# RMSNorm and a QKV projection: spent weight storage as output buffers, zero matmuls among the first transposes, a divided last product

## Chip, cores and metric

The kernel runs on one core of one Trainium2 chip. The metric is the device time of one launch in microseconds (us).

## The reference

Rows of x are divided by their root mean square, multiplied by gamma, and projected by a weight matrix.

```python
# x: (8, 1024, 768) float32, gamma: (768,), w_qkv: (768, 2304), eps = 1e-5
rms = np.sqrt(np.mean(x ** 2, axis=-1, keepdims=True) + eps)
x_norm = x / rms * gamma
return np.matmul(x_norm, w_qkv).astype(np.float32)
```

## The kernel before

The 8192 rows of x are 64 tiles of 128 rows. The inner dimension of 768 is six k-blocks of 128, and the 2304 output columns are three chunks `c` of 768.

**Start.** The weights arrive in 16 pieces (`load_w`). `conv` multiplies them by gamma and rounds them into one large bfloat16 tile, `w_b` (128 partitions x 6 x 2304, 27,648 bytes a partition). Tiles 0 to 3 of x are done in the plain way while the weights come in: `load_x`, `stat` (square sum and root on ScalarE), `cast` to bfloat16 on VectorE, `tr` (six transposes on TensorE into PSUM), `cp` (back to SBUF), `mm` (matmuls 512 or 256 columns wide against `w_b`, line 516), `evac` and `store`. `gamma_in` turns gamma into a column layout with one small transpose (line 549) and copies it to `g_sb` (line 550). `idle(n, nl)` issues n matmuls of zeros, nl columns wide, into a PSUM tile that nobody reads (line 555).

**Scaling.** For each chunk, `bound` and `fold` find the largest weight, `bound_tr`, `bound_top`, `bound_all` and `scales` make one scale of it and spread it over the partitions by way of TensorE (lines 585 and 595), and `quad` and `tsum` make eight scaled float16 blocks of weights, each 3 k-blocks by 384 columns. After the `quad`s of chunk 2 nothing reads `w_b` any more.

**The rest.** Tiles 4 to 63 are taken in pairs `p` = 2 to 31. A pair and a chunk form a 2x2 by 2x2 block product done with seven block products (the Winograd form of Strassen's scheme) in place of eight. `pstat`, `prms`, `precip` and `pcast` normalise a tile and round it to float16 (line 648), `pxbar` transposes it by DMA (for a few early tiles `ptr` does it on TensorE), and `osum` makes the four sums of blocks of x (line 666). `product` is three matmuls 384 columns wide (line 686), accumulated in one of three PSUM banks "a", "b", "c" of the pair and chunk. `hold` copies an intermediate sum to SBUF (lines 693 and 695), `join` adds a held sum to a bank and writes a part of the output tile (VectorE, line 704), and `last` writes the fourth part (ScalarE, line 708). `pstore` sends a part or a whole output tile of 768 columns to memory (SyncE's queue, line 714).

**Buffers.** `outp` holds 12 output tiles `ot` of 1024 float32, 4096 bytes a partition; `result` takes a new one for each tile and chunk. PSUM is a pool of eight tiles `pm` of one bank each. A buffer that is taken anew waits until everything that used it last is done, for an output tile its store.

**Order.** Nothing is reordered by a scheduler. `PLAN` is a list, written out, of (time, operation, arguments). The operations are called in order of these times, and each engine and queue runs its own instructions in the order of the calls; the times have no other effect. From pair 15 on (`STEADY`) the list is made by a loop with `when`. The last chunk of the last pair (`end`) has an order of its own:

```python
            for i, u in ((1, 0), (5, 1), (2, 7.5 if end else 2), (6, 4), (3, 5), (7, 7 if end else 10), (4, 8.5 if end else 13)):
                when(u, product, p, c, i)
```

The first entries of the list put `gamma_in` and six zero matmuls behind the first loads, and then the transposes of tiles 2, 1, 3 and 0, as x arrives.

Of the kernel before, what the change touches and what calls it, by code (L numbers as in the profile page):

```python
# [19 lines left out]
    (0.000, "load_x", 2), (4.040, "stat", 2), (4.041, "cast", 2, "DVE"), (4.042, "load_x", 1), (5.240, "stat", 1),  # L20
    (5.241, "load_x", 3), (5.242, "cast", 1, "DVE"), (5.243, "load_x", 0), (5.530, "recip", 2), (5.531, "load_w", 4),
    (5.532, "load_w", 1), (5.533, "load_w", 0), (5.534, "gamma_in"), (5.535, "idle", 6, 512), (5.536, "tr", 2),
    (8.470, "conv", 4, 5, "POOL"), (8.471, "cp", 2, "DVE"), (8.472, "cast", 3, "DVE"), (9.150, "conv", 1, 2, "POOL"),
    (9.151, "tr", 1), (9.152, "tr", 3), (9.153, "recip", 1), (9.154, "cast", 0, "DVE"), (9.155, "cp", 1, "ACT"),
    (9.156, "tr", 0), (9.157, "load_w", 3), (9.158, "cp", 0, "DVE"), (9.310, "mm", 1, 0, "5"), (9.311, "stat", 3),
    (9.526, "mm", 2, 0, "5"), (9.742, "mm", 0, 0, "5"), (9.743, "load_w", 2), (9.744, "load_w", 6),
    (9.745, "recip", 3), (9.990, "mm", 0, 0, "2"), (10.206, "mm", 1, 0, "2"), (10.451, "conv", 0, 0, "DVE"),
# [5 lines left out]
    (14.418, "load_w", 8), (14.419, "conv", 6, 3, "ACT"), (14.420, "mm", 0, 0, "01"), (14.421, "mm", 2, 0, "012"),  # L33
# [6 lines left out]
    (18.420, "mm", 3, 512, "45"), (18.421, "load_x", 5), (18.544, "bound_tr", 0), (18.545, "evac", 1, 512, "ACT"),  # L40
# [4 lines left out]
    (20.510, "mm", 3, 1024, "23"), (20.511, "scales", 0), (20.512, "evac", 3, 0, "DVE"),  # L45
    (20.942, "mm", 2, 1024, "23"), (21.374, "mm", 1, 1024, "45"), (21.375, "quad", 0, "b22", "ACT"),
    (21.376, "quad", 0, "b11", "POOL"), (21.377, "bound", 1, 1, "DVE"), (21.805, "mm", 2, 1024, "01"),
    (22.237, "mm", 3, 1024, "01"), (22.238, "load_w", 14), (22.239, "pstat", 4), (22.505, "pstat", 5),
    (22.669, "mm", 0, 1024, "45"), (22.670, "quad", 0, "b12", "POOL"), (22.994, "quad", 0, "b21", "POOL"),
    (23.101, "mm", 2, 512, "45"), (23.532, "mm", 1, 1024, "23"), (23.533, "bound", 1, 2, "DVE"),  # L50
    (23.534, "evac", 0, 512, "ACT"), (24.075, "prms", 2), (24.076, "mm", 2, 1024, "45"),
    (24.325, "conv", 14, 0, "ACT"), (24.755, "conv", 15, 4, "ACT"), (24.756, "mm", 3, 1024, "45"),
    (24.757, "conv", 14, 2, "POOL"), (24.758, "conv", 14, 1, "DVE"), (24.759, "fold", 1),
    (24.827, "mm", 1, 1024, "01"), (25.259, "bound_tr", 1), (25.260, "load_w", 13), (25.379, "mm", 1, 2048, "012"),
    (25.380, "precip", 2), (25.381, "evac", 2, 512, "DVE"), (25.579, "bound_top", 1), (25.707, "mm", 2, 2048, "012"),
    (26.034, "mm", 3, 2048, "012"), (26.362, "bound_all", 1), (26.363, "conv", 15, 5, "POOL"), (26.364, "pcast", 4),
    (26.365, "conv", 15, 3, "ACT"), (26.366, "evac", 3, 1024, "ACT"), (26.614, "pcast", 5),
    (26.615, "conv", 13, 4, "POOL"), (27.164, "conv", 13, 5, "DVE"), (27.165, "load_x", 7),
    (27.166, "evac", 2, 1024, "ACT"), (27.167, "pstat", 7), (27.168, "mm", 3, 2048, "345"), (27.169, "load_w", 12),
    (27.170, "mm", 2, 2048, "345"), (27.171, "load_w", 11), (27.594, "scales", 1), (27.595, "load_x", 6),  # L60
    (27.785, "evac", 2, 2048, "ACT"), (27.786, "mm", 1, 2048, "345"), (27.787, "mm", 0, 2048, "012"),
    (27.788, "load_x", 26), (28.175, "evac", 1, 2048, "ACT"), (28.315, "store", 2, 2, 2048, 256),
    (28.316, "quad", 1, "b21", "POOL"), (28.317, "mm", 0, 2048, "345"), (28.318, "tsum", 0, "t1", "DVE"),
    (28.319, "ptr", 5), (28.614, "evac", 3, 2048, "DVE"), (28.615, "ptr", 4), (29.014, "evac", 0, 2048, "DVE"),
    (29.414, "evac", 1, 1024, "DVE"), (30.074, "pcp", 4, "DVE"), (30.075, "store", 1, 2, 2048, 256),
    (30.076, "quad", 1, "b11", "ACT"), (30.077, "mm", 2, 1536, "45"), (30.078, "conv", 12, 3, "ACT"),
    (30.079, "mm", 3, 1536, "45"), (30.080, "mm", 0, 1536, "45"), (30.081, "load_x", 17), (30.574, "pcp", 5, "DVE"),
    (30.575, "mm", 1, 1536, "45"), (30.576, "conv", 11, 1, "ACT"), (30.577, "conv", 12, 2, "POOL"),
    (30.578, "mm", 0, 1024, "23"), (31.074, "bound", 2, 1, "DVE"), (31.075, "mm", 0, 1024, "01"),
    (31.429, "product", 2, 0, 1), (31.430, "conv", 11, 0, "POOL"), (31.431, "pstat", 6),  # L70
# [4 lines left out]
    (34.108, "store", 3, 2, 2048, 256), (34.109, "store", 0, 2, 2048, 256), (34.110, "quad", 1, "b12", "POOL"),  # L75
    (34.111, "mm", 1, 1536, "01"), (34.112, "mm", 3, 1536, "01"), (34.507, "mm", 1, 1536, "23"),
    (34.939, "mm", 0, 1536, "23"), (34.940, "pcast", 7), (35.370, "product", 2, 1, 1),
    (35.371, "tsum", 0, "t2", "DVE"), (35.372, "evac", 3, 1536, "ACT"), (35.904, "osum", 2, "s2", "DVE"),
    (36.058, "hold", 2, 1, "a", "p1", "ACT"), (36.364, "osum", 2, "s4", "POOL"), (36.365, "tsum", 1, "t1", "DVE"),
    (36.366, "ptr", 6), (36.367, "ptr", 7), (36.558, "pcp", 6, "ACT"), (36.559, "load_x", 8),  # L80
    (36.924, "pcp", 7, "DVE"), (37.424, "evac", 0, 1536, "DVE"), (37.425, "product", 2, 0, 5),
    (37.426, "product", 2, 1, 2), (37.427, "hold", 2, 0, "c", "p5", "ACT"), (37.428, "load_x", 13),
    (37.553, "product", 2, 0, 6), (37.878, "bound", 2, 2, "ACT"), (38.084, "tsum", 1, "t2", "DVE"),
    (38.085, "product", 3, 0, 1), (38.784, "tsum", 0, "t3", "DVE"), (38.785, "product", 2, 1, 5),
    (39.484, "osum", 2, "s3", "DVE"), (39.485, "product", 2, 0, 3), (39.804, "osum", 3, "s1", "DVE"),
    (39.805, "hold", 2, 0, "a", "u2", "ACT"), (39.806, "load_x", 15), (40.264, "osum", 3, "s2", "POOL"),
    (40.265, "tsum", 0, "t4", "DVE"), (40.266, "product", 3, 1, 1), (40.267, "hold", 2, 1, "c", "p5", "ACT"),
    (40.478, "evac", 1, 1536, "ACT"), (41.794, "osum", 3, "s3", "POOL"), (41.795, "join", 2, 1, 0, 0, "b", "p1"),
    (41.796, "product", 2, 1, 6), (41.797, "fold", 2), (41.798, "product", 2, 0, 7), (41.799, "product", 2, 1, 3),
    (41.800, "join", 2, 0, 0, 1, "c", "u2"), (42.074, "join", 2, 0, 1, 1, "a", "p5"), (42.075, "load_x", 9),  # L90
    (42.076, "product", 3, 0, 5), (42.077, "hold", 3, 1, "a", "p1", "ACT"), (42.078, "bound_tr", 2),
    (42.079, "hold", 3, 0, "a", "p1", "ACT"), (42.080, "product", 3, 1, 6), (42.081, "pstat", 9),
    (42.548, "product", 2, 0, 2), (43.035, "product", 2, 0, 4), (43.036, "bound_top", 2), (43.523, "bound_all", 2),
    (43.524, "load_x", 12), (43.643, "product", 3, 0, 6), (43.644, "hold", 2, 1, "a", "u2", "ACT"),
    (43.645, "tsum", 1, "t3", "DVE"), (43.646, "tsum", 1, "t4", "DVE"), (43.647, "hold", 3, 1, "a", "u2", "ACT"),
    (43.648, "load_x", 11), (44.244, "join", 2, 1, 0, 1, "c", "u2"), (44.794, "scales", 2),
    (44.795, "osum", 3, "s4", "POOL"), (44.796, "load_x", 10), (44.797, "product", 2, 1, 7),
    (45.114, "join", 2, 1, 1, 1, "a", "p5"), (45.664, "join", 2, 0, 0, 0, "b", "p1"), (45.665, "product", 3, 1, 7),
    (45.666, "pstat", 8), (45.667, "product", 3, 1, 2), (45.668, "product", 3, 1, 5),
    (45.669, "store", 1, 0, 0, 1024), (45.670, "hold", 3, 0, "c", "p5", "ACT"),  # L100
# [3 lines left out]
    (47.865, "prms", 4), (48.030, "product", 3, 1, 3), (48.031, "store", 3, 0, 0, 1024),  # L104
# [3 lines left out]
    (48.519, "product", 2, 2, 1), (49.064, "join", 3, 0, 1, 1, "a", "p5"), (49.065, "pstat", 10),  # L108
    (49.066, "store", 3, 1, 1024, 1024), (49.067, "product", 3, 1, 4), (49.068, "pstore", 2, 0, 0),
    (49.408, "last", 2, 1), (49.908, "last", 3, 1), (49.909, "pstore", 2, 1, 0), (49.910, "product", 3, 2, 1),  # L110
    (49.911, "pcast", 9), (49.980, "product", 3, 0, 4), (50.164, "tsum", 2, "t1", "DVE"), (50.468, "ptr", 9),
    (50.668, "last", 3, 0), (51.168, "hold", 2, 2, "a", "p1", "ACT"), (51.668, "pcp", 9, "ACT"), (51.669, "pcast", 8),
    (51.670, "product", 3, 2, 2), (51.671, "tsum", 2, "t2", "DVE"), (52.488, "hold", 3, 2, "a", "p1", "ACT"),
    (52.489, "product", 2, 2, 2), (52.490, "ptr", 8), (52.491, "product", 2, 2, 6), (52.492, "pstore", 2, 0, 1),
# [254 lines left out]
def kernel(  # L369
# [327 lines left out]
    def result(p, c, i, j):  # L697
        t = 2 * p + i
        if (t, "s", c) not in OUT:
            OUT[t, "s", c] = outp.tile([P, 1024], f32, name="ot")  # L700
# [106 lines left out]
```

## Time and profile before

| | |
|---|---|
| time, median of 3 runs | 356.48 us (355.76, 356.48, 357.01) |
| time of the profiled execution | 356.93 us |
| its span, first to last instruction | 354.8 us |
| mean granted TensorE clock | 0.995 |
| TensorE (PE) busy | 343.6 us, 97% |
| VectorE (DVE) busy | 267.8 us, 75% |
| ScalarE (ACT) busy | 243.7 us, 69% |
| GpSimd (POOL) busy | 116.9 us, 33% |
| data moved by DMA | 117.8 MB, 332 GB/s on average |

The profile is of one execution. PEld is the loading of TensorE's stationary operand, which overlaps its matmuls; SP is SyncE, whose queue issues nearly all DMAs. A row of the timeline has start, duration, engine, line, operation, what is written and read, and in brackets the engine's idle time before it with what ended that. A row of waits has who waited for whom, the us in total, how many times, and the longest. A row of the table of stretches has the stretch, its length, then busy us (and instructions) of PE, PEld, DVE, ACT and POOL, the granted clock, the DMA engines' share and the GB/s moved. A matmul's duration in the trace is longer than the distance to the next one, since matmuls are pipelined; the distance of their starts is the time that one costs.

### The profile page before, as it was taken

The page shows a single profiled execution, that of the slowest core. Times are in us where ns is not written, and L with a number is a line of the kernel's source. Part 1 is how long each engine was busy: PE and PEld are TensorE (multiplying, and loading weights), DVE is VectorE, ACT ScalarE, POOL GpSimd, SP SyncE. Part 2 cuts the span into 40 slices and gives each one's busy share as a digit, 9 for nine tenths or more (in the row PEclk, how much of TensorE's full clock was granted, in tenths as well). Part 3 has the DMA queues.
Part 4 walks back from the last instruction along what each step waited for, and adds up shares of the span by engine and source line. Part 5 has one row for each costly group of instructions (what it writes and reads, how often), then busy time and mean ns, then how long its engine had stood idle before and what let it go on. Part 6 is the DMA issues. An engine that isn't in the chain of part 4 may idle for free.

```text
span 354.8 us, 6638 instructions
## 1 busy us (share of the span) xinstructions
PE 343.6 (97%) x2113; PEld 203.6 (57%) x2113; DVE 267.8 (75%) x504; ACT 243.7 (69%) x498; POOL 116.9 (33%) x135
## 2 busy tenths in 40 slices
PE   5999999999999999999899999999999999999995
PEld 2446566666665656655456566565666656566562
DVE  3689999788778878887676868677777867676663
ACT  6798989878885557656457667676767677665543
POOL 0396444222233303650254080613407061444000
PEclk9899999999999999999999999999999999999999
DMA  7999999999998999999999999999999999987565
GB/s 267 389 381 307 360 416 345 400 347 378 324 393 254 303 361 329 282 350 396 320 332 371 255 380 353 366 334 304 365 360 383 333 327 343 313 305 262 208 266 222
DMA packets 80493, 117.80 MB, mean 332 GB/s; under 512 B 43590, under 2 KB 45388, under 8 KB 80460
## 3 DMA queue, kind: packets, MB, share of 16 engines
q1 hardware_dynamic: 80448, 117.40, 99.1%
q8 instruction: 16, 0.26, 0.3%
q14 instruction: 17, 0.14, 0.1%
q10 hardware_dynamic: 12, 0.00, 0.0%
HBM read 32.25 MB, written 75.50 MB: 304 GB/s over the span
## 4 chain that ended last, share of the span: by engine, by line
PE 54%; DVE 1%; ACT 0%; issue 0%
PE pm L686 54%; DVE ot L704 1%; DVE xb L648 0%; ACT ot L708 0%; DVE pp L693 0%
## 5 line engine op out<-in xcount | busy, mean ns | idle before, releaser
L686 PE MATMUL pm<-wq,su 128*128 128x384 f16 x1080 | 204.9, 326 | 0.8 <-DVE ot L704 0.8
L704 DVE SCALAR_TENSOR_TENSOR ot<-pm,sc,pp 128x384 f32<-128x384 f32 x270 | 156.6, 613 | 47.6 <-PE pm L686 42.3
L695 ACT ACTIVATE pp<-pm,sc 128x384 f32<-128x384 f32 x203 | 114.0, 582 | 75.3 <-PE pm L686 71.9
L686 PE MATMUL pm<-wq,xT 128*128 128x384 f16 x810 | 160.9, 326 | 1.7 <-DVE ot L704 1.5
L686 PEld LDWEIGHTS <-su 128*128 128x128 f16 x1080 | 105.2, 98 | 70.1 <-issue 1.2
L686 PEld LDWEIGHTS <-xT 128*128 128x128 f16 x810 | 79.1, 98 | 54.7 <-issue 2.6
L666 POOL TENSOR_TENSOR su<-xT 128x384 f16<-128x384 f16 x51 | 46.3, 925 | 154.3 <-PE pm L686 84.9
L708 ACT ACTIVATE ot<-pm,sc 128x384 f32<-128x384 f32 x90 | 51.8, 577 | 25.5 <-PE pm L686 24.9
L693 DVE TENSOR_SCALAR pp<-pm,sc 128x384 f32<-128x384 f32 x67 | 40.9, 616 | 23.5 <-PE pm L686 23.0
L634 ACT ACTIVATE sq<-x_t 128x768 bf16<-128x768 f32 x60 | 50.3, 838 | 0.1
L648 DVE TENSOR_SCALAR xb<-x_t,rstd 128x768 f16<-128x768 f32 x60 | 40.3, 678 | 0.4
L666 POOL TENSOR_TENSOR su<-su,xT 128x384 f16<-128x384 f16 x27 | 25.3, 938 | 26.5 <-DVE su L666 14.6
L666 POOL TENSOR_TENSOR su<-xT,su 128x384 f16<-128x384 f16 x27 | 25.2, 935 | 10.0 <-DVE su L666 6.7
L516 PE MATMUL pm<-w_b,xT 128*128 128x512 bf16 (+1 forms) x120 | 26.2, 375 | 0.4 <-POOL w_b L452 0.4
L516 PEld LDWEIGHTS <-xT 128*128 128x128 bf16 x120 | 11.8, 101 | 12.5 <-issue 2.7
L452 POOL TENSOR_SCALAR w_b<-wq,g_sb 128x512 bf16<-128x512 f32 (+1 forms) x14 | 9.1, 662 | 14.0 <-DMA wq<-in_w_qkv_dram 14.0
L618 POOL TENSOR_SCALAR wq<-w_b,inv 128x1152 f16<-128x1152 bf16 x9 | 11.2, 1261 | 4.9 <-DVE inv L602 4.9
L634 ACT ACTIVATION_READ_ACCUMULATOR sq<-x_t 128x1 f32 x60 | 11.7, 195 | 0.0
L624 DVE TENSOR_TENSOR wq<-wq 128x1152 f16<-128x1152 f16 x12 | 9.2, 785 | 0.0
L573 DVE TENSOR_REDUCE bnd<-w_b 128x1 f32<-128x1536 bf16 x5 | 8.7, 1747 | 0.3 <-ACT w_b L450 0.3
L638 ACT ACTIVATE rms<-ssq,eps_sb 128x2 f32<-128x2 f32 x30 | 8.8, 294 | 0.0
L534 ACT ACTIVATE ot<-pm,rstd 128x512 f32<-128x512 f32 x10 | 6.6, 684 | 1.1 <-PE pm L516 1.0
(48 smaller groups left out, 79.3 us busy)
## 6 DMA issues: line engine op xcount, KB each, us to landing
out_dram<-ot SPq DMA_DIRECT2D x178, 384.0 KB, 4.6
x_t<-in_x_dram SPq DMA_DIRECT2D x64, 384.0 KB, 5.4
wq<-in_w_qkv_dram SPq DMA_DIRECT2D x10, 512.0 KB, 9.1
out_dram<-ot SPq DMA_DIRECT2D x8, 512.0 KB, 9.3
wq<-in_w_qkv_dram SPq DMA_DIRECT2D x4, 256.0 KB, 6.8
xT<-xb SPq DMA_TRANSPOSE x49, 5.0
wq<-in_w_qkv_dram SPq DMA_DIRECT2D x2, 384.0 KB, 9.7
out_dram<-ot SPq DMA_DIRECT2D x4, 192.0 KB, 2.3
```

The source lines that it names most:

```text
L452: nc.gpsimd.tensor_scalar(out=o, in0=i, scalar1=g, scalar2=1.0, op0=mult, op1=mult)
L516: nc.tensor.matmul(out=PM[t, n0][:, :nl], lhsT=XT[t][:, ko, :], rhs=w_b[:, ko, n0:n0 + nl], start=(b == 1), stop=(b == KO))
L618: nc.gpsimd.tensor_scalar(out=o, in0=quad_view(c, q), scalar1=INV[c], scalar2=1.0, op0=mult, op1=mult)
L624: (nc.vector if eng == "DVE" else nc.gpsimd).tensor_tensor(out=new_quad(c, q), in0=i0, in1=i1, op=sub)
L634: nc.scalar.activation(out=sq, in_=X[t], func=AF.Square, accum_out=SS[p][:, t % 2:t % 2 + 1])
L648: nc.vector.tensor_scalar(out=XB[t], in0=X[t], scalar1=SS[t // 2][:, t % 2:t % 2 + 1], scalar2=None, op0=mult)
L666: (nc.vector if eng == "DVE" else nc.gpsimd).tensor_tensor(out=block(p, q), in0=block(p, x), in1=block(p, y), op=op)
L686: nc.tensor.matmul(out=PB[k][:, :CW], lhsT=block(p, a)[:, ko, :], rhs=WQ[c, b][:, ko, :], start=(first and ko == 0), stop=(ko == KO // 2 - ...
L693: nc.vector.tensor_scalar(out=o, in0=pb, scalar1=SC[c], scalar2=None, op0=mult)
L695: nc.scalar.activation(out=o, in_=pb, func=AF.Copy, scale=SC[c], bias=0.0)
L704: nc.vector.scalar_tensor_tensor(out=result(p, c, i, j), in0=PB[p, c, bank][:, :CW], scalar=SC[c], in1=PART[p, c, held], op0=mult, op1=add)
L708: nc.scalar.activation(out=result(p, c, 1, 0), in_=PB[p, c, "a"][:, :CW], func=AF.Copy, scale=SC[c], bias=0.0)
```

## The change

Three things change. First, the list's beginning: `gamma_in` and the six zero matmuls are called ahead of the first load, and six more zero matmuls are called after the transposes of tile 1, two after those of tile 3 and two after those of tile 0 (the list's other entries are written differently, 8.47 for 8.470, and are the same). Second, from pair 4 on the output tiles of chunk 2, and of chunk 1 for the second tile of every even pair, are put into `w_b`, whose bytes are taken as nine slots of 768 float32 in turn; this is 70 output tiles, and `outp` still has 12 buffers for the others. Third, the last product of all is computed in two halves of 192 columns, drained by VectorE and ScalarE, and each half has a store of its own, from SyncE's and from ScalarE's queue.

```diff
 PLAN = [
-    (0.000, "load_x", 2), ...
+    (2.4, "gamma_in"), (2.7, "idle", 6, 512), (2.701, "load_x", 2), ...
...
-    ... (5.534, "gamma_in"), (5.535, "idle", 6, 512), (5.536, "tr", 2),
+    ... (5.534, "tr", 2),
...
-    (9.151, "tr", 1), (9.152, "tr", 3), (9.153, "recip", 1), (9.154, "cast", 0, "DVE"), (9.155, "cp", 1, "ACT"),
-    (9.156, "tr", 0), (9.157, "load_w", 3), ...
+    (9.151, "tr", 1), (9.1514, "idle", 6, 512), (9.152, "tr", 3), (9.1524, "idle", 2, 512), (9.153, "recip", 1),
+    (9.154, "cast", 0, "DVE"), (9.155, "cp", 1, "ACT"), (9.156, "tr", 0), (9.1564, "idle", 2, 512),
+    (9.157, "load_w", 3), ...
...
+    spare = []
+
     def result(p, c, i, j):
         t = 2 * p + i
         if (t, "s", c) not in OUT:
-            OUT[t, "s", c] = outp.tile([P, 1024], f32, name="ot")
+            if p >= 4 and (c == 2 or (c == 1 and i == 1 and p % 2 == 0)):
+                s = 2 * CW * (len(spare) % (KO * N // (4 * CW)))
+                spare.append((t, c))
+                OUT[t, "s", c] = w_b.rearrange("p k n -> p (k n)").bitcast(f32)[:, s:s + 2 * CW]
+            else:
+                OUT[t, "s", c] = outp.tile([P, 1024], f32, name="ot")
...
+    def end_piece(p, c, h):
+        w = CW // 2
+        k = (p, c, "a")
+        a, b = PRODUCTS[4]
+        for ko in range(KO // 2):
+            nc.tensor.matmul(out=PB[k][:, w * h:w * (h + 1)], lhsT=block(p, a)[:, ko, :], rhs=WQ[c, b][:, ko, w * h:w * (h + 1)],
+                             start=False, stop=(ko == KO // 2 - 1), skip_group_check=True)
+
+    def end_out(p, c, h):
+        w = CW // 2
+        t = 2 * p + 1
+        o, pb = result(p, c, 1, 0)[:, w * h:w * (h + 1)], PB[p, c, "a"][:, w * h:w * (h + 1)]
+        if h == 0:
+            nc.vector.tensor_scalar(out=o, in0=pb, scalar1=SC[c], scalar2=None, op0=mult)
+        else:
+            nc.scalar.activation(out=o, in_=pb, func=AF.Copy, scale=SC[c], bias=0.0)
+        n0 = 2 * CW * c + w * h
+        (nc.sync if h == 0 else nc.scalar).dma_start(out=of[t * P:(t + 1) * P, n0:n0 + w], in_=o)
...
-            for i, u in (..., (4, 8.5 if end else 13)):
-                when(u, product, p, c, i)
+            for i, u in (..., (4, 13)):
+                if not (end and i == 4):
+                    when(u, product, p, c, i)
...
-                when(9.7, last, p, c)
-                when(10.6, pstore, p, c, 1, 0)
+                when(8.5, end_piece, p, c, 0)
+                when(8.6, end_piece, p, c, 1)
+                when(9.7, end_out, p, c, 0)
+                when(9.8, end_out, p, c, 1)
```

## The prediction

> **What bounds the kernel now.** I read the page first: busy shares and the clock row.
>
> ```profile
> PE 343.6 (97%) x2113; PEld 203.6 (57%) x2113; DVE 267.8 (75%) x504; ACT 243.7 (69%) x498; POOL 116.9 (33%) x135
> ...
> PEclk9899999999999999999999999999999999999999
> ...
> DMA  7999999999998999999999999999999999987565
> ```
>
> TensorE is the bound, so only time in which it stands idle or runs slowly can be won. The granted clock drops only in the second slice (8.9 to 17.7 us). Next, the table of stretches, cut where the clock changes and then by stage.
>
> ```profile
> 3.47:6.88 3.41, 2.96 (x16) 1.68 (x14) 1.81 (x5) 2.76 (x7) 0.00 (x0) 1.00 0.93 312
> 6.88:10.29 3.41, 1.18 (x13) 0.83 (x14) 1.76 (x5) 2.74 (x7) 0.91 (x2) 1.00 1.05 395
> 10.29:13.71 3.42, 3.42 (x9) 1.21 (x8) 2.05 (x6) 2.30 (x3) 0.45 (x1) 0.50 1.05 389
> 13.71:17.12 3.41, 3.41 (x17) 1.56 (x16) 2.58 (x3) 2.42 (x4) 1.36 (x2) 1.00 1.05 388
> ...
> 33.00:153.00 120.00, 120.00 (x768) 72.46 (x766) 103.05 (x199) 91.36 (x189) 40.65 (x42) 1.00 1.04 346
> 153.00:179.00 26.00, 23.77 (x143) 13.90 (x143) 19.17 (x35) 14.24 (x30) 7.13 (x8) 1.00 1.08 353
> 179.00:350.00 171.00, 171.00 (x1053) 102.83 (x1052) 122.25 (x225) 111.27 (x232) 53.45 (x60) 1.00 0.97 320
> ```
>
> The first figure after the stretch is its length, the next TensorE's busy time. After a stretch with 1.18 us of work comes one at clock 0.50, in which TensorE is busy throughout but gets through 9 matmuls instead of 17. From 33 to 153 us and from 179 to 350 us it is never idle. In between it loses 2.2 us; the chain of waits there runs through the casts of x (line 648) and evictions on VectorE, with no DMA in it. The 1.00 of the first row stands for want of an earlier clock record: transposes start 0.107 us apart up to 6.12 and 0.056 apart from 8.2, so the start ran at half clock too, and the stretch of 2.96 us earned the full one. The timeline of the start shows what stands around the thin stretch.
>
> ```profile
> 2.41 2.75 PE L555 MATMUL pm<-const-float32-0.0 128*128 128x512 bf16 x6
> 4.95 1.49 PE L480 MATMUL pm<-ident,xb 128*128 128x128 bf16 x12
> 8.21 0.51 PE L480 MATMUL pm<-ident,xb 128*128 128x128 bf16 x6 [1.77 <-DVE xb L456]
> 9.17 0.51 PE L480 MATMUL pm<-ident,xb 128*128 128x128 bf16 x6 [0.46 <-DVE xb L456]
> 10.12 10.05 PE L516 MATMUL pm<-w_b,xT 128*128 128x512 bf16 x38 [0.44 <-POOL w_b L452]
> ```
>
> The gaps wait for x tiles, cast on VectorE as they land. Last, three rows of the waits, and then the last product with its eviction:
>
> ```profile
> PE pm L686 <- DVE ot L704: 2.3, 4, 0.8
> ...
> ACT ot L708 <- DMA out_dram<-ot: 0.4, 1, 0.4
> DVE ot L704 <- DMA out_dram<-ot: 0.4, 1, 0.4
> ```
>
> ```profile
> 350.27 0.65 PE L686 MATMUL pm<-wq,xT 128*128 128x384 f16 x3 [0.22 <-DVE ot L704]
> ...
> 350.96 0.58 ACT L708 ACTIVATE ot<-pm,sc 128x384 f32<-128x384 f32 x1 [1.27 <-PE pm L686]
> ```
>
> Stores hold up an eviction twice in the whole run, 0.4 us each, both inside stretches in which TensorE lost nothing.
>
> **What the Trainium skill says.** "TensorE: Matmul & The Clock Gate", Part 1 (What's actually happening): the half clock is the default, activity lifts it, and activity is judged in windows of about 3.4 us that run free of the kernel. The trace agrees: the half-clock stretch is 3.42 us long. The same page (Why this matters for your kernels) warns of idle gaps over about 3 us; here the longest gap is 1.77 us and the clock fell all the same, after a window 35% busy (1.18 of 3.41), so the measurement decides: it is the share. "PSUM — Partial Sum Buffer", section on bank collisions: no two engines may touch one bank at once, two readers included. No run here shows a collision; it tells why the built program has the waits named below. "DMA: Bandwidth & Descriptors", Anatomy of one DMA: most of a transfer's cost is a fixed part, its receipt, though given for another issuing path. The trace's quiet final stores agree: 1.8 to 2.4 us from issue to landing, whatever they queue behind.
>
> **The change, part by part.**
>
> *Zeros.* Six zero matmuls now follow the transposes of tile 1, two those of tile 3, two those of tile 0. At full clock one takes 0.216 us, at half 0.427 (spacing of the 512-wide matmuls after and before 13.71). With this execution's windows: the last transpose leaves at 6.22; 0.66 us remain at half clock (1.5 matmuls), the other 4.5 take 0.97, to 7.85, while tile 3 is ready at 8.21. The next pair fills 8.55 to 8.98 (tile 0 at 9.17), the last 9.52 to 9.95 (weights at 10.12). So they delay nothing by 0.36, 0.19 and 0.17 us, and the stretch from 6.88 gets 0.97 + 0.43 + 0.43 = 1.83 us more work: 3.0 of 3.41, 88%, as much as the 2.96 that had earned the full clock one window earlier. The clock should stay up.
> Gain: eight matmuls at 0.427 instead of 0.216 are 8 x 0.211 = 1.69 us. Not all can be cashed, as the weights come late: VectorE's conversion of k-block 3 ends at 13.12 and its first matmul starts at 13.96, so with 0.05 of hand-over 0.79 is the most. Further on VectorE's `fold` ends at 19.32 (0.15 us from 19.17) and its transpose starts at 20.10: 0.73. That wait does not depend on TensorE, and it is late next. After it the bounds move along with TensorE's own results, and from 33 us TensorE is full. I take **-0.7**, bounds -1.7 (weights early) and 0 (clock falls anyway).
>
> *gamma first.* Its transpose and the first six zeros stood there already on TensorE. VectorE's copy `g_sb` (0.14 us) moves ahead of the first cast: queued behind it are the casts, and behind those the transposes. gamma lands by 2.24, x not before 3.85, VectorE idles until then: 0. Were gamma later than x, the casts would be late by the difference.
>
> *PSUM.* Three more zero tiles take turns among eight banks. The next user waits for zeros that are done: 0 (at most 0.2).
>
> *Output buffers.* From pair 4 on 70 of 188 large output tiles move to nine slots in `w_b`; twelve `ot` buffers serve the other 118. Queue orders stay as they were, SyncE's too. In the built program each eviction waits for the store of its own slot alone. The last reader of `w_b` (POOL, line 618) ends at 50.7 us, the first slot is written about 67; on the times of before a slot's last store had landed at least 13.8 us ahead of reuse. Both 0.4 us waits go, and evictions stood before TensorE's need: **0**, bounds -0.8 and +0.3 (stores in the slots contending).
>
> *Last product.* Three 384-wide matmuls become six 192-wide: 3 x 0.163 = 0.49 against 6 x 0.0825 = 0.50. The result is drained by VectorE and ScalarE, one half each. But both halves lie in one bank, and in the built program VectorE's half waits for the sixth matmul and **ScalarE's half waits for VectorE's**. VectorE: 256 columns 0.478, 384 0.616, so 192 about 0.41; ScalarE (0.470, 0.577) about 0.42. From 350.97 that is 351.38, then 351.42 to 351.84, where before ScalarE ended at 351.54: +0.30. Then ScalarE issues 96 KB itself (queued behind that: nothing). Its one issue before took 0.57 us against 0.33 on SyncE: up to +0.2. Half the bytes: 96 KB at 236 to 320 GB/s is -0.3 to -0.4 (estimate from the stretch table). Before: issue 351.57, landed 353.69. Sum **+0.1**, bounds -0.3 and +0.5.
>
> Sum: -0.7 + 0 + 0 + 0.1 = -0.6. The profiled execution took 356.93 (span 354.8 and 2.13 around it): 356.3. It stands 0.45 above the median, 356.48; the fastest run, 355.76, may have had its windows in a better place and would gain nothing from the zeros: 355.9. I put the median between: **356.0**.
>
> **Rivals.** *A, the forecast:* zeros worth up to 0.7, buffers nothing, end nothing: 355.4 to 356.4.
> *B, nothing:* the clock falls all the same, or most runs kept it; against it the 88%, for it the free-running windows: 356.3 to 356.9.
> *C, the buffers matter:* other executions may hold evictions for stores longer than the one profiled, or the 2.2 us lost between 153 and 179 go with them. For it: DMA shares near 1. Against it: that chain has no DMA. With all 2.2 us gone 356.0 becomes 353.8, with a third of it 355.3: 353.8 to 355.3.
> *D, slower: the zeros stand in the way at half clock.* If the window that would raise the clock ends late, six zeros take 2.56 us, to 8.78, 0.57 past tile 3; then 0.64 of transposes, 0.85, 0.64 and 0.85 put the first real matmul at 11.77 instead of 10.12. At half clock up to 13.71 it does 4.5 matmuls by then and reaches the eleventh at 14.9 instead of 13.96: +0.95, with the end's +0.3 about 357.7. It decides if the clock is still half at 8.2 us. For it: the pairs have only 0.19 and 0.17 us to spare. Against it: zeros are activity too, and raise the clock at the next boundary.
>
> **Numbers.** A 0.58, B 0.15, C 0.15, D 0.12. 0.3%, 1.07 us, is about what a measurement here tells from no change. Faster by more (under 355.41): C, and A's rim, 0.20; within: 0.68; slower (over 357.55): D, 0.12. The range takes in A, B and half of C and of D: 354.9 to 357.4.
>
> **What would show it.** Right: the clock at 1.00 from about 7 us on, matmuls 0.216 us apart at 11 us, the `fold` transpose waiting for VectorE near 19.4; no wait for `out_dram` stores, yet the same 120.00 of 120.00 busy; at the end ScalarE starting after VectorE. Wrong: evictions of `w_b` waiting for DMAs, TensorE losses gone around 153 to 179 us, or a half clock past 10 us.

## The result and the profile after

As forecast, the change makes no difference of 0.3% or more, which is what the forecast counted as clear. In the first comparison the median is 356.24 us (356.00 to 356.83, four runs) beside 356.12 us for the kernel before (355.73 to 357.01, four runs): a ratio of 1.0002, interval 0.9978 to 1.0027. Two later comparisons of the same kernel gave 0.9991 [0.9981, 1.0001] and 0.9985 [0.9975, 0.9995]. Over all of them the mean is 355.89 us (48 executions) beside 356.14 us (the 160 executions of before that stood beside the experiments): 0.25 us less, 0.07%.

The profiled execution took 356.00 us, its span is 354.1 us (before 354.8). In the code after, lines move by one in the head (516 is now 515) and by six around `join` and `last` (704 is 710, 708 is 714).

The page first: busy shares, the clock row and the DMA row.

```profile
PE 344.9 (97%) x2123; PEld 204.4 (58%) x2126; DVE 268.2 (76%) x505; ACT 243.5 (69%) x498; POOL 119.3 (34%) x135
...
PEclk9999999999999999999999999999999999999999
...
DMA  7999999999998998999999999999999999977565
```

The 8 in the second slice of the clock row is gone. The table of stretches, cut as before, with one row more, shows what changed (stretch, length, busy us and instructions of PE, PEld, DVE, ACT and POOL, clock, DMA share, GB/s).

```profile
3.47:6.88 3.41, 3.26 (x18) 1.80 (x16) 1.65 (x4) 2.51 (x7) 0.00 (x0) 1.00 0.88 290
6.88:10.29 3.41, 3.37 (x22) 1.50 (x21) 1.47 (x4) 3.10 (x7) 0.62 (x1) 1.00 1.03 384
10.29:13.71 3.42, 2.85 (x12) 1.10 (x12) 2.19 (x7) 2.01 (x2) 0.73 (x2) 1.00 1.05 395
13.71:17.12 3.41, 3.41 (x18) 1.52 (x17) 2.44 (x4) 2.31 (x6) 1.36 (x2) 1.00 1.05 387
...
7.74:11.15 3.41, 3.36 (x24) 1.55 (x23) 1.82 (x5) 2.35 (x6) 1.36 (x2) 1.00 1.04 390
...
33.00:153.00 120.00, 119.92 (x769) 72.53 (x767) 103.45 (x200) 91.17 (x187) 40.15 (x42) 1.00 1.04 347
153.00:179.00 26.00, 24.25 (x147) 14.21 (x146) 19.03 (x35) 14.24 (x30) 7.83 (x9) 1.00 1.08 355
179.00:350.00 171.00, 170.78 (x1054) 102.78 (x1052) 122.41 (x225) 111.38 (x232) 53.83 (x60) 1.00 0.97 320
```

The stretch from 6.88 holds 3.37 us of work instead of 1.18, and the one behind it runs at 1.00 instead of 0.50. The clock's own windows lie elsewhere in this execution: the zeros start 0.427 us apart up to 7.44 and 0.22 apart from 7.81, so the clock rose near 7.74 us, and the window from there is busy for 3.36 of 3.41 us. But in the stretch from 10.29 TensorE is busy in only 2.85 of 3.42 us: where it had been slow, it now waits. From 33 us on it is nearly as full as before (119.92 of 120.00 us, 170.78 of 171.00), and the stretch from 153 to 179 us still loses 1.75 us. The timeline of the start shows the new wait.

```profile
8.47 0.51 PE L479 MATMUL pm<-ident,xb 128*128 128x128 bf16 x6
8.82 0.60 PE L554 MATMUL pm<-const-float32-0.0 128*128 128x512 bf16 x2
9.46 0.51 PE L479 MATMUL pm<-ident,xb 128*128 128x128 bf16 x6
9.81 0.60 PE L554 MATMUL pm<-const-float32-0.0 128*128 128x512 bf16 x2
10.41 1.26 PE L515 MATMUL pm<-w_b,xT 128*128 128x512 bf16 x5
12.17 7.48 PE L515 MATMUL pm<-w_b,xT 128*128 128x512 bf16 x32 [0.50 <-DVE w_b L447]
19.66 0.22 PE L584 MATMUL pm<-ident,bmax 128*1 128x128 bf16 x1
```

Five real matmuls go by at full speed, and the sixth waits for VectorE's conversion of weights (line 447): the distance of the starts is 0.66 us longer than 0.216. That conversion had itself waited for its load. The transpose after `fold` starts at 19.66 instead of 20.10, so this execution won 0.44 us in the head, with a first real matmul that came 0.29 later (10.41 against 10.12): GpSimd's first conversion, for which it waits, ended at 10.36 instead of 10.07, because its weights landed later.

No row of the waits names an eviction that waits for an `out_dram` store any more. The last rows of the timeline give the divided end.

```profile
349.44 0.66 PE L721 MATMUL pm<-wq,xT 128*128 128x192 f16 x6 [0.22 <-DVE w_b L710]
...
350.13 0.42 DVE L729 TENSOR_SCALAR w_b<-pm,sc 128x192 f32<-128x192 f32 x1 [0.22 <-PE pm L721]
350.57 0.33 SPq L733 DMA_DIRECT2D out_dram<-w_b  x1
350.58 0.42 ACT L731 ACTIVATE w_b<-pm,sc 128x192 f32<-128x192 f32 x1 [1.73 <-DVE w_b L729]
351.03 0.38 ACTq L733 DMA_DIRECT2D out_dram<-w_b  x1
```

ScalarE's half starts 0.03 us after VectorE's has ended. From the start of the last product to the end of the span it is 4.70 us; before it was 4.52. So the 0.65 us by which this span is shorter are, within 0.02, the head (-0.44), a loss near 153 us that is 0.24 instead of 0.65 and has another cause (below), and the end (+0.18).

### The profile page after: what moved, and what is told of

The parts are those of the page before. It is cut to its first block, busy times and chain, and to the rows that moved or that the text cites. A ratio compares the mean times of both kernels' runs of the same rounds, so it can differ in the third digit from the quotient of the medians.

```text
span 354.1 us, 6615 instructions
## 1 busy us (share of the span) xinstructions
PE 344.9 (97%) x2123; PEld 204.4 (58%) x2126; DVE 268.2 (76%) x505; ACT 243.5 (69%) x498; POOL 119.3 (34%) x135
## 4 chain that ended last, share of the span: by engine, by line
PE 93%; DMA 2%; DVE 2%; SPq 1%; issue 0%; ACT 0%; DVEq 0%
PE pm L685 86%; PE pm L515 6%; DMA wq<-in_w_qkv_dram 2%; PE pm L670 1%; DVE w_b L710 1%; SPq L436 0%; DVE pp L692 0%; DVE xb L647 0%; SPq L441 0%; PE pm L721 0%; ACT w_b L714 0%; PE pm L584 0%; DVE w_b L447 0%; DVE w_b L729 0%; ACT w_b L731 0%
## 5 line engine op out<-in xcount | busy, mean ns | idle before, releaser
L710 DVE SCALAR_TENSOR_TENSOR ot<-pm,sc,pp 128x384 f32<-128x384 f32 x172 | 101.1, 611 | 28.1 <-PE pm L685 24.7
L665 POOL TENSOR_TENSOR su<-xT 128x384 f16<-128x384 f16 x51 | 46.3, 924 | 152.6 <-PE pm L685 93.6
L710 DVE SCALAR_TENSOR_TENSOR w_b<-pm,sc,pp 128x384 f32<-128x384 f32 x98 | 58.5, 614 | 19.5 <-PE pm L685 18.0
L714 ACT ACTIVATE ot<-pm,sc 128x384 f32<-128x384 f32 x48 | 27.7, 577 | 12.1 <-PE pm L685 12.0
L714 ACT ACTIVATE w_b<-pm,sc 128x384 f32<-128x384 f32 x41 | 23.7, 577 | 11.7 <-PE pm L685 11.6
L515 PE MATMUL pm<-w_b,xT 128*128 128x512 bf16 (+1 forms) x117 | 24.7, 357 | 0.7 <-DVE w_b L447 0.5
L451 POOL TENSOR_SCALAR w_b<-wq,g_sb 128x512 bf16<-128x512 f32 (+1 forms) x14 | 10.6, 764 | 14.9 <-DMA wq<-in_w_qkv_dram 14.9
```

What stands on the lines that cost most here:

```text
L451: nc.gpsimd.tensor_scalar(out=o, in0=i, scalar1=g, scalar2=1.0, op0=mult, op1=mult)
L515: nc.tensor.matmul(out=PM[t, n0][:, :nl], lhsT=XT[t][:, ko, :], rhs=w_b[:, ko, n0:n0 + nl], start=(b == 1), stop=(b == KO))
L665: (nc.vector if eng == "DVE" else nc.gpsimd).tensor_tensor(out=block(p, q), in0=block(p, x), in1=block(p, y), op=op)
L710: nc.vector.scalar_tensor_tensor(out=result(p, c, i, j), in0=PB[p, c, bank][:, :CW], scalar=SC[c], in1=PART[p, c, held], op0=mult, op1=add)
L714: nc.scalar.activation(out=result(p, c, 1, 0), in_=PB[p, c, "a"][:, :CW], func=AF.Copy, scale=SC[c], bias=0.0)
```

## The experiments

Three questions: what each part is worth alone, whether the parts' values add up, and where the 0.25 us come from. Each kernel was compared with the kernel before on the same chip. Beside the ratios I use the mean span over the executions, with its standard error, and the mean time outside the span (device time minus span).

### Each part alone

`e1_zeros_only`: the list of the change in the kernel before.

```diff
+    (2.4, "gamma_in"), (2.7, "idle", 6, 512), (2.701, "load_x", 2), ...
+    (9.151, "tr", 1), (9.1514, "idle", 6, 512), (9.152, "tr", 3), (9.1524, "idle", 2, 512), ...
+    (9.156, "tr", 0), (9.1564, "idle", 2, 512),
```

> The kernel before with the new beginning of the list alone (gamma first, ten more zero matmuls). Theory 1 (the clock windows run free): no execution shows a half clock after about 8 us, mean granted clock 0.998 or more in each, while executions of the kernel before fall into two kinds, clock about 0.995 with a half-clock stretch near 10 us and clock 0.998 or more without one; the zeros win 0.4 to 0.7 us over the first kind and nothing over the second, so the medians differ by 0 to 0.6 us, ratio 0.998 to 1.000. Theory 2 (the profiled execution of before was late for another reason): all executions of before show about the same clock, and the medians agree within 0.2 us. Theory 3 (the zeros win in every execution and another part gives it back): 355.4 us or less, ratio 0.998 or less with an interval below 1.

Measured: 355.84 us, ratio 0.9996 [0.9985, 1.0007], mean span 353.71 +- 0.12 beside 353.89 +- 0.09. In the profile the clock is full from 5.26 us on, and the sixth matmul waits 0.68 us for weights. No execution of the 14 had a mean granted clock of 0.996 or less; 22 of 51 of the kernel before had. The value of 0.995 is one window of 3.41 us at half clock (3.41 x 0.5 of 354 us is 0.005). Values down to 0.997, which stood against the 0.998 expected, come without one: the clock also falls behind the last matmuls (in the first trace of the change at 352.49 us), and that counts. So no drop in mid-run is left, as expected, and what the zeros win is small.

`e4_no_zeros`: the kernel before without its six zeros.

```diff
-    ... (5.534, "gamma_in"), (5.535, "idle", 6, 512), (5.536, "tr", 2),
+    ... (5.534, "gamma_in"), (5.536, "tr", 2),
```

> The kernel before without its own six zero matmuls at the start. Theory 1 (the share of work in a window of 3.4 us earns the clock): the transposes before 7 us and the first real matmuls from about 10 us run at half clock (0.107 and 0.427 us apart) in every execution until about 13.7 to 14 us or one window earlier or later, mean clock 0.990 to 0.995, and the time is 0 to 0.6 us above the median of before. Theory 2 (the start does not matter, the weights' arrival hides it): within 0.1 us of before, whatever the clock does.

Measured: 356.23 us, 1.0009 [0.9997, 1.0022], mean span 354.10 +- 0.14. TensorE runs at half speed until 15.09 us, as the timeline of its start and a row of its stretches show:

```profile
4.61 1.79 PE L480 MATMUL pm<-ident,xb 128*128 128x128 bf16 x12 [2.17 <-DVE xb L456]
7.07 0.82 PE L480 MATMUL pm<-ident,xb 128*128 128x128 bf16 x6 [0.67 <-DVE xb L456]
9.05 0.82 PE L480 MATMUL pm<-ident,xb 128*128 128x128 bf16 x6 [1.16 <-DVE xb L456]
9.96 7.21 PE L516 MATMUL pm<-w_b,xT 128*128 128x512 bf16 x21
...
10.29:13.71 3.42, 3.42 (x9) 1.13 (x8) 2.24 (x7) 2.30 (x3) 0.29 (x1) 1.00 1.05 392
```

All transposes and the first real matmuls are slow: 9 matmuls in the stretch from 10.29, as at half clock before. Yet the row says 1.00, and the mean clock of this execution is 1.000; of all 22 it is 0.997 or more, where 0.990 to 0.995 was expected. The profile's clock starts with its first rise, and what lay before counts as full. So a mean clock near 1 tells that the clock did not fall again in mid-run, not that it was full from the start. In time the half clock costs 0.21 us on average, with an uncertainty of 0.17: most of it lies in time in which the weights aren't there.

`e2_buffers_only`: `result` with the slots in `w_b`, nothing else.

```diff
+            if p >= 4 and (c == 2 or (c == 1 and i == 1 and p % 2 == 0)):
+                ...
+                OUT[t, "s", c] = w_b.rearrange("p k n -> p (k n)").bitcast(f32)[:, s:s + 2 * CW]
```

> The kernel before with the nine slots in the spent weights alone. Theory 1: same time within 0.2 us; no wait of an eviction for a store is left in the profile, and TensorE still loses its 2 to 3 us between 150 and 179 us. Theory 3a (the slots cost time): 0.5 us slower or more, with evictions of w_b longer than those of ot (0.614 us) or waiting for DMAs. Rival C of the prediction (stores matter in other executions): 0.5 us or more faster.

Measured: 355.42 us, 0.9980 [0.9969, 0.9992]; mean span 353.50 +- 0.13, time outside the span 1.84 us instead of 2.15. By itself this reads as if the slots won 0.4 us inside the span and 0.3 outside. The second number came back in every kernel with slots, the first did not (below). Its head, which is that of before, kept the clock in the profiled execution: the window from 7.58 us, where the clock rose, was busy for 2.12 of 3.41 us (62%, where 35% had been too little before).

```profile
7.58:10.99 3.41, 2.12 (x17) 1.21 (x18) 1.44 (x5) 2.84 (x7) 1.36 (x2) 1.00 1.04 390
```

`e3_end_only`: the divided last product in the kernel before.

```diff
...
-                when(9.7, last, p, c)
-                when(10.6, pstore, p, c, 1, 0)
+                when(8.5, end_piece, p, c, 0)
+                when(8.6, end_piece, p, c, 1)
+                when(9.7, end_out, p, c, 0)
+                when(9.8, end_out, p, c, 1)
```

> The kernel before with the divided last product alone. Theory 1: from the start of the last product to the end of the span 4.6 to 4.8 us where before has 4.5 (354.8 less 350.27), since ScalarE's half starts only when VectorE's has ended: 0.1 to 0.3 us slower, ratio 1.0000 to 1.0010. Rival (both halves drain side by side and half the bytes land sooner): 4.1 us or less.

Measured: 355.97 us, 0.9994 [0.9979, 1.0009]; mean span 353.99 +- 0.20; from the last product to the end of the span 4.55 us; outside the span 1.86. Nothing lost and nothing won that can be told. Its head is that of before, too, and here the clock rose late, though the mean clock reads 1.000:

```profile
8.20 0.82 PE L480 MATMUL pm<-ident,xb 128*128 128x128 bf16 x6 [0.45 <-DVE xb L456]
9.12 9.68 PE L516 MATMUL pm<-w_b,xT 128*128 128x512 bf16 x38
```

The transposes take 0.82 us instead of 0.51, and the real matmuls start 0.427 us apart up to 11.64.

### Are twelve buffers enough?

`f4_nine_bufs` is the kernel before with three output buffers fewer.

```diff
-    outp = ctx.enter_context(tc.tile_pool(name="outp", bufs=12))
+    outp = ctx.enter_context(tc.tile_pool(name="outp", bufs=9))
```

> The kernel before with 9 output buffers in place of 12. If waits for stores cost time in the kernel before (the slots win by taking them away), fewer buffers cost more: evictions waiting for stores add up to several us on VectorE and ScalarE and the span grows by 0.5 us or more. If the eviction engines have room for such waits and the slots' gain came otherwise, the waits grow and the span stays within 0.3 us of 353.9.

Measured: 360.89 us, 1.0129 [1.0105, 1.0152]. Its rows of waits for stores:

```profile
DVE ot L704 <- DMA out_dram<-ot: 4.4, 2, 2.9
ACT ot L708 <- DMA out_dram<-ot: 1.1, 3, 0.4
```

And its table of stretches around them:

```profile
41.68:45.09 3.41, 1.51 (x10) 0.66 (x8) 0.62 (x1) 1.24 (x4) 1.63 (x2) 1.00 1.02 417
45.09:48.50 3.41, 2.42 (x8) 0.79 (x8) 2.10 (x5) 1.93 (x4) 0.00 (x0) 0.50 1.02 416
...
33.00:45.09 12.09, 10.19 (x67) 5.74 (x65) 8.44 (x18) 9.47 (x19) 4.78 (x5) 1.00 1.03 374
45.09:51.92 6.83, 5.84 (x19) 2.45 (x19) 4.44 (x10) 4.77 (x10) 2.50 (x3) 0.50 0.61 249
51.92:153.00 101.08, 101.08 (x651) 61.73 (x649) 84.96 (x164) 75.01 (x157) 28.42 (x31) 1.00 1.02 336
```

Two evictions wait 4.4 us for stores early in the pair stage, TensorE stands behind them for 2.07 us at 45.0 and 1.19 at 47.1 (distances of starts, less what a matmul costs at the clock of that time), and the clock falls to half from 45.09 to 51.92, which costs more on top. ScalarE's three waits, from 343 us on, cost TensorE nothing. All this is before pair 4's slots could help: they are first written at about 67 us. So nine buffers are too few around 45 us, where the change adds none, and enough later, where it adds nine. Twelve lose nothing at either place; how near to the edge they are was not measured.

### The time outside the span

The kernel before stood at 2.15 us outside the span, `e1` and `e4` at 2.16 and 2.11, `e2` and `e3` at 1.84 and 1.86. I suspected the number of instructions that ScalarE executes. `f1_one_more_act` issues one activation more than before:

```diff
+    nc.scalar.activation(out=tbl, in_=eps_sb, func=AF.Sqrt)
```

> The kernel before with its small table-loading activation on ScalarE issued twice (0.2 us, at about 2.8 us, where ScalarE idles until 3.85). It computes the same. In the runs so far the device time is 2.13 to 2.16 us longer than the span in the kernel before and the two that change TensorE's instructions alone, and 1.84 to 1.86 us in the three whose ScalarE program has another number of instructions (744 against 731, 746 and 733). If that number decides, one instruction more (745) gives a time outside the span of about 1.85 us with the same span of 353.9: 0.3 us faster. If something else decides (the slots, the second store queue), it stays at 2.15 us and the time is the same.

Measured: 355.93 us, 0.9996 [0.9983, 1.0009], outside the span 2.15. The theory fell.

### Do the parts add up? Twice each

`f2_after_again` is the whole change; `f3_zeros_buffers` is the change with the last product as before.

> The changed kernel once more, beside the others on one chip. If its parts add up (time outside the span -0.3, slots -0.4 of span, zeros -0.2, divided end +0.1), it is 355.2 to 355.5 us where before has 356.0, ratio 0.998 with an interval below 1, and the first comparison, of four runs each, was too coarse to see it. If the slots' gain of the second experiment was a draw, or the parts do not add, 355.7 to 356.2, ratio 0.999 to 1.001.

> The changed kernel with the undivided last product of before. Against the changed kernel itself it shows the end alone: 0.1 to 0.2 us less from the start of the last product to the end of the span (4.5 against 4.7) if the serial drain costs what the trace says. Against the kernel with zeros alone (span 353.7 on average) it shows the slots alone: 353.3 if they are worth 0.4 us of span, 353.7 if they are worth nothing.

Measured: the whole change 356.06 us, 0.9991 [0.9981, 1.0001], mean span 354.21 +- 0.11; without the divided end 355.60 us, 0.9973 [0.9961, 0.9986], 353.62 +- 0.12. That reads as if the divided end cost 0.6 us and the rest beat both kernels. The traces did not bear it out: 4.71 us from the last product on against 4.64. So both were run again, on the other chip, with a third kernel. `g3_split_store` drains the last product undivided, by ScalarE alone, and only stores it in halves from two queues:

```diff
-                when(10.6, pstore, p, c, 1, 0)
+                when(10.6, half_store, p, c, 0)     # 192 columns, SyncE's queue
+                when(10.7, half_store, p, c, 1)     # 192 columns, ScalarE's queue
```

> The change with the last product undivided (as in before), a second time, on the same chip and beside the two kernels that follow. Earlier its mean span was 353.62 us +- 0.12, that of the whole change 354.21 +- 0.11, a difference of 0.59 +- 0.16, while in the traces the divided end costs only 0.07 us from the start of the last product on. Theory P, the divided end costs what the traces show: the mean span of this kernel lies within 0.3 us of that of the whole change in these runs. Theory M, it costs 0.6 us in most executions: the span lies 0.4 to 0.8 us below, about 353.6 against 354.2. Either way the time outside the span is 1.85 us, and the median 355.4 to 355.8.

> The whole change once more. P: mean span 353.6 to 353.9 us, within 0.3 of the kernel with the undivided end. M: about 354.2, 0.4 to 0.8 above it. Time outside the span 1.85 us, median 355.6 to 356.1 and ratio 0.998 to 1.000.

> Zeros and slots, the last product undivided and drained by ScalarE alone as before, but its 384 columns are stored in two halves of 192, one from SyncE's queue and one from ScalarE's. It keeps the second queue and the halved store of the divided end and takes away the two halves drained one after the other. If the second queue or the half stores are what the end costs: the span is that of the whole change, 4.7 us from the start of the last product to the end of the span and a mean of 354.1 to 354.3 under M. If the serial drain costs it: 4.45 to 4.6 us, and the mean span is that of the undivided end or up to 0.2 less, 353.4 to 353.7.

Measured: 356.19 us, 0.9994 [0.9981, 1.0007], mean span 354.30 +- 0.18 without the divided end; 355.66 us, 0.9985 [0.9975, 0.9995], 353.81 +- 0.11 with it; 355.90 us, 0.9996 [0.9985, 1.0006], 354.11 +- 0.11 with the split store. The order turned round. Both theories had a size for the difference, and neither a negative one; what holds is that the same kernel differs between two comparisons by 0.4 us (the change) and 0.7 us (without the divided end), well beyond its standard errors. Pooled, the span is 354.01 us with the divided end (44 executions) and 354.05 without (35): no difference. No version among these beats the kernel before by more than 0.3%.

In the traces, from the last product to the end of the span, the end agrees within 0.02 us from trace to trace of the same form:

| last product | results in `outp` | results in slots |
|---|---|---|
| undivided | 4.51 to 4.52 (five traces) | 4.62 to 4.64 (three) |
| divided | 4.55 (`e3`) | 4.70 to 4.71 (three) |
| undivided, stored in halves | | 4.72 (`g3`) |

So 0.11 of the 0.18 us come with the slots: the last 192 KB land 2.24 to 2.25 us after their issue instead of 2.12 to 2.13. Why, no run shows. The divided end costs 0.03 us without slots and 0.07 with them, and the halved stores alone cost about as much, without any serial drain.

All the kernels, with mean span and mean time outside it:

| kernel | zeros | slots | divided end | mean span (executions) | outside |
|---|---|---|---|---|---|
| before, three comparisons | | | | 353.89 (51), 354.01 (50), 354.05 (59) | 2.15 |
| e1 | yes | | | 353.71 (14) | 2.16 |
| e2 | | yes | | 353.50 (14) | 1.84 |
| e3 | | | yes | 353.99 (14) | 1.86 |
| e4, no zeros at all | | | | 354.10 (22) | 2.11 |
| f1, one activation more | | | | 353.81 (22) | 2.15 |
| f3, g1 | yes | yes | | 353.62 (13), 354.30 (22) | 1.86, 1.85 |
| g3 | yes | yes | stores only | 354.11 (22) | 1.84 |
| f2, g2: the change | yes | yes | yes | 354.21 (22), 353.81 (22) | 1.83, 1.84 |
| f4, nine buffers | | | | 359.28 (6) | 1.84 |

## Why the prediction was right, and where its steps were not

The total held: forecast 356.0 us and no measurable change. Step by step:

**Luck in the number.** The forecast took 0.48 us off a median of 356.48, of three runs. Beside the change, before had 356.12, and 356.14 on average over 160 executions: the starting point was high, and 356.0 was met without the gain that was to lead there.

**What bounds the kernel.** Right from 33 us on: TensorE was the limit before and after, but for 0.08 us of the long stretch up to 153 us and 0.22 of the one from 179. In the head it was not: there the weights are the limit as soon as the clock is full.

**The zeros, as a mechanism.** Right. In all seven traces of kernels with all the zeros the clock rises between 5.26 and 7.80 us and stays up until the last matmuls, and none of their 119 executions has a mean clock of 0.996 or less, as 70 of 160 of the kernel before have. The count alone would not show it, since the kernel with no zeros at all has none either, for want of an early rise. In the first trace the zeros stand in nobody's way: the last two are through at 10.24 (9.81 + 0.43), and the first real matmul starts at 10.41. In three others they do (rival D, below).

**The zeros, as a size.** For the profiled execution the sum was right. The trace of after has 37 of the 38 real matmuls ahead of `fold`'s transpose; the record between 12.77 and 13.20 us is missing (twice 0.215). So the eleventh is the one at 13.45, 0.05 us behind VectorE's third conversion (12.91 + 0.49), and it comes 3.04 us after the first real matmul instead of 3.84: 0.80 won, where 0.79 was the most. Then `fold`:

```profile
19.46 0.15 DVE L579 TENSOR_REDUCE bmax<-bnd 128x1 bf16<-128x3 f32 x1
```

Its transpose at 19.66 starts 0.05 us after it, where 0.78 had passed in before: 0.73, as forecast. Only the weights, which landed 0.29 us later in this execution, made 0.44 of it.

The mis-sized term is the step from this execution to the median: the prediction took the middle between two ends, where the share of executions was to be weighed. `fold`'s transpose shows it. In all ten traces in which the clock is full by the first real matmul it starts 0.05 or 0.06 us after `fold` has ended, and in eight of them 9.28 to 9.31 us after GpSimd's first conversion, with the new zeros or without them (`e2`, `f1` and `f4` have the head of before): the weights set the time, and nothing is left to win. Of the five traces with the head of before, three are of this kind, before itself loses 0.73 and `e3`, with its late rise, 0.40. An estimate from these five is 0.23 us on average for the zeros. The counts agree: the 70 executions of before with a low clock have a mean span of 354.20 us, the other 90 of 353.82, so removing the low clock alone is worth 70/160 x 0.38 = 0.17 us; the late rises come on top, as they hide among the 90. Measured, the zeros alone gave 0.17 us with an uncertainty of 0.15. The whole change gives up 0.18 of it again at the end, and its span is the same, 354.05 +- 0.08 against 353.98 +- 0.05. With comparisons differing by 0.4 to 0.7 us this fits, but doesn't prove it.

**gamma first, PSUM: 0.** No wait in the trace of after names either beyond what stood there before.

**Output buffers: 0.** In the pair stage this stands: the waits for stores went, as said, and TensorE is about as full as before. At the end of the span it doesn't quite: +0.11, within the bound of +0.3. Evictions into the slots take as long as into the pool's buffers (rows of the costliest groups, profile after: 614 and 611 ns):

```profile
L710 DVE SCALAR_TENSOR_TENSOR ot<-pm,sc,pp 128x384 f32<-128x384 f32 x172 | 101.1, 611 | 28.1 <-PE pm L685 24.7
L710 DVE SCALAR_TENSOR_TENSOR w_b<-pm,sc,pp 128x384 f32<-128x384 f32 x98 | 58.5, 614 | 19.5 <-PE pm L685 18.0
```

What was not foreseen is the time outside the span, 0.31 us less: it is more than the whole 0.25 us of the mean. It comes with the slots (1.83 to 1.86 in every kernel that has them), but also with the divided end alone and with nine buffers. What these have in common is open; the trace doesn't reach to either side of the span.

**A loss that seemed to go.** The prediction named losses gone between 153 and 179 us as a sign against it. The first of them, at 153.5 us in before and 152.6 after, fell from 0.65 to 0.24 us in the first trace, and it looked like the slots' doing. It isn't gone with them: it is 0.66, 0.45, 0.25 and three times nothing in other traces of kernels with slots. It follows the cast of x (line 647) on VectorE, and that follows GpSimd's sums (line 665). Timeline of the whole change, second comparison (no loss):

```profile
149.66 0.91 POOL L665 TENSOR_TENSOR su<-su,xT 128x384 f16<-128x384 f16 x1
150.59 0.61 DVE L647 TENSOR_SCALAR xb<-x_t,rstd 128x768 f16<-128x768 f32 x1
150.65 2.19 POOL L665 TENSOR_TENSOR su<-xT,su 128x384 f16<-128x384 f16 x2
151.78 1.14 PE L685 MATMUL pm<-wq,xT 128*128 128x384 f16 x6
```

And of the kernel without the divided end, its second comparison (0.66 us lost):

```profile
151.23 2.10 POOL L665 TENSOR_TENSOR su<-xT,su 128x384 f16<-128x384 f16 x2
151.30 1.25 DVE L647 TENSOR_SCALAR xb<-x_t,rstd 128x768 f16<-128x768 f32 x1
...
153.13 1.14 PE L685 MATMUL pm<-wq,xT 128*128 128x384 f16 x6 [0.49 <-DVE w_b L710]
```

In the first the cast starts 0.06 us ahead of a sum, takes 0.61 us, and TensorE's matmuls run on at 151.78. In the second it starts 0.07 us behind one and takes 1.25; the evictions queue behind it, and TensorE waits for them. In the twelve traces other than that of nine buffers TensorE's loss here is the cast's time less 0.60 us, within 0.01: casts of 0.84, 1.05, 1.13 and 1.25 go with losses of 0.24, 0.45, 0.53 and 0.65. The five of them without slots all lose 0.36 to 0.65; whether slots shift the meeting of the two engines on average stays open. The other losses, 0.16, 0.95, 0.94 and 0.35 us, from 164 to 178 us in the first trace, are the same within 0.01 us in all thirteen traces.

**The divided end: +0.1.** Right in sum, +0.07 beside the undivided end with slots; the rest of the +0.18 is the slots'. The serial drain was right: ScalarE ends 1.56 us after the last product's start instead of 1.27, +0.29 (predicted +0.30). Half the bytes gave less than said: the last 96 KB took 2.02 us from the start of their issue to the landing (351.03 to 353.05), 192 KB from a slot 2.25, so -0.23 instead of -0.3 to -0.4. The issue's +0.2 did not come: it took 0.38 us, hardly more than SyncE's 0.33. 0.29 - 0.23 = 0.06. The split store has no serial drain: its halves were issued together at 350.69 and landed 2.1 and 2.3 us later, the later one no sooner than 192 KB undivided.

**The rivals.** B, nothing, came nearest for the mean span, but how many runs kept the clock isn't known: 90 of 160 show no fall in mid-run, and those with a late rise are among them. C, the buffers, showed in `f4` at 45 us, but not where the slots are; and where other executions with twelve buffers hold an eviction longer, as ScalarE stands for 0.88 us behind a store at 181 us in `e1` and `f1`, TensorE loses nothing. D, the zeros in the way, did occur, though not at its size. The third comparison's trace of the change:

```profile
6.22 2.25 PE L554 MATMUL pm<-const-float32-0.0 128*128 128x512 bf16 x6
6.66 0.56 DVE L455 CAST xb<-x_t 128x768 bf16<-128x768 f32 x1 [0.28 <-DMA x_t<-in_x_dram]
8.31 0.50 PE L479 MATMUL pm<-ident,xb 128*128 128x128 bf16 x6
8.49 1.40 POOL L451 TENSOR_SCALAR w_b<-wq,g_sb 128x512 bf16<-128x512 f32 x2 [7.06 <-DMA wq<-in_w_qkv_dram]
...
9.85 8.74 PE L515 MATMUL pm<-w_b,xT 128*128 128x512 bf16 x38
18.60 0.22 PE L584 MATMUL pm<-ident,bmax 128*1 128x128 bf16 x1
```

x came sooner here: tile 3 is cast by 7.22, but the six zeros, the first four at half clock, hold its transposes until 8.31. GpSimd's first conversion is done at 9.18, and the first real matmul comes only at 9.85. In `f3` it is late by 0.77 us and in `g3` by 0.2. None of this cost anything in the end: the matmuls behind wait less for weights (the sixth 0.19 us, the eighth 0.16), and `fold`'s transpose starts 0.06 us after `fold` as in the others.

## What to carry to other kernels

Raising the clock of an engine that next waits for data only turns slow work into idle time, so find the first instruction behind it that waits for something else, and weigh what is left by the share of executions that had the low clock. Read that share from the distances of matmul starts too, since a mean clock near 1 can hide a slow start. Before adding buffers, look for a stretch where evictions wait for stores and TensorE waits for the evictions; here memory that happened to come free elsewhere took two short waits away and won nothing inside the span. And repeat a comparison of a few tenths of a per cent, runs of both kernels and all, before believing it: an interval of 0.9961 to 0.9986 became 0.9981 to 1.0007 for the same kernel.

## What the runs showed of the hardware

**VectorE's cast waits for a running GpSimd sum.** In the eleven of those twelve traces in which this cast starts while a sum is running, it takes 0.42 us more than what is left of that sum, and at least 0.60: 0.83 us left gave 1.25, 0.62 gave 1.05, 0.43 gave 0.84, 0.15 gave 0.60. The cast grows with what is left of the sum, so it is a wait rather than a slower cast. In turn, the sum that started 0.06 us after a cast took 1.32 us instead of 0.91. The Trainium skill says this of the two engines ("SBUF — State Buffer", section "SBUF: two separate sides"): they share a pair of ports as an exclusive lock, held for the whole instruction by whoever comes first, if VectorE's instruction runs in a mode with two ports or has two inputs in SBUF. No trace names the mode of this cast; the times in both directions agree with such a lock. An offset of 0.13 us between two engines near 151 us (0.06 ahead, 0.07 behind) thus decides 0.66 us of TensorE's time.

**The clock falls in mid-run too, and a window busy for 71% at half clock did not lift it.** With nine buffers the window from 41.68 us was busy for 1.51 of 3.41 us (44%), and the clock went to half for 6.83 us, two windows: the first of them, busy for 2.42 us (71%) at half clock, did not lift it. In `e3` a window at half clock busy for 2.46 us (5.00 to 8.41) did not either, and the next, with 3.31, did. At full clock 2.12 us (`e2`) and 2.09 (`f1`) were enough to keep it. What lies between 44% and 61% was not measured.

**Time outside the span has two levels.** 2.11 to 2.16 us or 1.83 to 1.86 us, fixed for each kernel over all its executions (1.78 to 1.91 for one group, 2.07 to 2.24 for the other), and not a matter of one ScalarE instruction more or less.
